# A two-layer decoder trunk on one core: fixed order of the first stage, and gemvs moved from the first FFN into the SSM

## The chip, the cores and the metric

The program runs on one core of one Trainium2 chip. A core has five engines that run side by side and meet at semaphores: TensorE (PE) for matrix products, VectorE (DVE), ScalarE (ACT) and GpSimd (POOL) for work on elements, and SyncE (SP), whose queue issues the transfers from memory in its own order. The metric is the device time of one execution in microseconds; lower is better. The kernel before takes 1230.64 us, the median of three runs between 1229.85 and 1232.05.

## The reference

A sequence of 512 tokens with 1024 channels passes two layers. Each layer has a token mixer (stick-breaking attention in layer 0, a diagonal complex state-space model, the SSM, in layer 1) and a gated feed-forward net (FFN) with a causal convolution of width 3. A vector c conditions every step: its silu times a large matrix gives shift, scale and gate vectors. All is float32.

```python
c_act = jax.nn.silu(c)
for i in range(DEPTH):
    mod = c_act @ w_mod[i] + b_mod[i]
    sh1, sc1, g1, sh2, sc2, g2 = jnp.split(mod, 6, axis=-1)
    h = modulate(rms_norm(x, norm_mix[i]), sh1, sc1)
    ...
        y = stick_breaking_attention(h, w_qkv[j], w_o_attn[j])
    ...
        y = s5_ssm(h, w_in_ssm[j], ...)
    x = x + g1[:, None, :] * y
    h = modulate(rms_norm(x, norm_ffn[i]), sh2, sc2)
    x = x + g2[:, None, :] * conv_ffn(h, w_up[i], conv_w[i], conv_b[i], w_down[i])
```

A norm divides each token by its root mean square, and `modulate` is h * (1 + scale) + shift.

## The kernel before

x lies channel-wise: eight tiles x[k] of 128 channels x 512 tokens. A float32 product is made of three products of rounded parts: `mm3` (lines 145, 148, 149) takes high x high, low x high and high x low. So each weight tile is loaded (`..._r`), copied to its high part by ACT (`..._h`, line 139), and its low part is the difference, by DVE (`..._l`, line 140). Activations have parts too: hH and hL after a norm, gH and gL after the gating of the FFN.

The stages follow one another: the first stage (load x, silu of c, squares, statistics, conditioning, and v = h times w_v over k = 0 to 7), attention in windows, the product with w_o, FFN0 in groups of 8, 8 and 6 pairs of up products, each group followed by a down projection dn_0, dn_1, dn_2, the SSM with its glu and output product, and FFN1. While FFN0 runs, POOL and the SP queue prepare the matrices of the SSM (`ssm_prep`, in pieces by `pace`).

**First stage.** `rstd_y` makes statistics: products of the sum of squares `acc` with ones (line 237), a square root on ACT, and five small DVE instructions (lines 242 to 246). `rstd_stat` puts the result on diagonals `dg` (line 254), and a product of dg with ones (line 490) broadcasts it over the partitions as `rbc`. The squares (line 1163) are summed on DVE (line 1165). Statistics are made for tokens 0 to 255, then again for 256 to 511. `norm_tile` multiplies x by the broadcast (nt, line 277), ACT makes hH and the affine value (lines 280, 281), and DVE makes hL (line 282). Shift and scale of the first norm come from gemvs: one DVE instruction multiplies 128x1024 weights by the broadcast `cact` and sums each row (`gemv_step`, line 170), two for each k, with weights in four slots `wgs`.

**Background gemvs.** All later conditioning vectors come from a list `bgq`; `bg(n)` takes the next n gemvs from it, and a vector's eight gemvs are followed by a final (`gemv_fin`, line 176). Their weights (`wg`) have two buffers, so SP can load a gemv's weights only when the one before last is done. In FFN0 gemvs stand behind pairs and in the down projections (`after`).

**Order.** A scheduler with a timeline of its own decides the order of instructions on each engine, apart from those held in program order (`keep_in_program_order`, `pe_pin`, `behind_head`). Each engine takes its list strictly in order, and the SP queue too: a load that waits for a buffer holds all loads behind it. The norms of the other stages go through `head_mm`, which starts the next stage's products on the first half of the tokens before the statistics of the second half.

## Time and profile before

| | |
|---|---|
| median of three runs | 1230.64 us |
| profiled execution | 1229.2 us |
| its span | 1227.2 us |
| PE busy | 1170.5 us (95%), 6136 instructions |
| DVE busy | 871.8 us (71%) |
| ACT busy | 562.6 us (46%) |
| POOL busy | 259.6 us (21%) |
| granted clock of PE, mean | 0.987 |

A row of the profile names an engine, the line of the kernel, the operation and its tiles (out<-in). The wait view says for whom an engine stood idle. The granted clock is a share of TensorE's full 2.4 GHz. PE is busy nearly throughout, so it is its few idle stretches, and those at a lower rate, that are looked for.

### The profile page before, as it was taken

The numbers are of one execution on the slowest core, as the hardware profiler recorded it, in microseconds if no ns is written. First come the engines' busy times: TensorE is split into PE (matmuls) and PEld (weight loads), VectorE is DVE, ScalarE is ACT, GpSimd is POOL, SyncE is SP. The second block draws the span as 40 slices with busy tenths as digits, with TensorE's granted clock in tenths as the row PEclk, the third lists the DMA queues.
The fourth block names the chain that finished last, engine by engine and source line by source line (L and its number), as shares of the span: only waits on it lengthen the run. The fifth ranks groups of instructions, "written<-read, shape, count | busy, mean of one in ns | idle before, by whom it ended". The sixth has DMA issues, their size and how long they took to land.

```text
span 1227.2 us, 16428 instructions
## 1 busy us (share of the span) xinstructions
PE 1170.5 (95%) x6136; PEld 959.5 (78%) x6136; DVE 871.8 (71%) x1305; ACT 562.6 (46%) x891; POOL 259.6 (21%) x241
## 2 busy tenths in 40 slices
PE   6999999899999999779999899999999999999997
PEld 4777776588888788558887888789888888888887
DVE  7868888747984778787678658566698458744645
ACT  7656656346642123331335657653653234422434
POOL 1000000000197986959740000000000000000003
PEclk9999999899999999979999899999999999999999
DMA  9774656521434876877767579332255436433211
GB/s 338 279 238 143 209 172 193 149 96 53 138 94 152 266 229 209 253 232 236 231 190 236 180 231 346 118 103 87 70 189 205 134 123 194 157 96 103 82 56 69
DMA packets 93395, 211.01 MB, mean 172 GB/s; under 512 B 19586, under 2 KB 39682, under 8 KB 93315
## 3 DMA queue, kind: packets, MB, share of 16 engines
q1 hardware_dynamic: 84994, 207.86, 52.8%
q10 hardware_dynamic: 8320, 2.10, 0.8%
q8 instruction: 48, 0.79, 0.3%
q14 instruction: 33, 0.26, 0.1%
HBM read 188.68 MB, written 21.24 MB: 171 GB/s over the span
## 4 chain that ended last, share of the span: by engine, by line
PE 61%; DVE 21%; POOL 5%; issue 4%; ACT 4%; DMA 4%; SPq 0%; POOLq 0%; ACTq 0%; DVEq 0%
PE up L148 8%; PE up L149 8%; PE up L145 7%; PE dn L145 4%; PE dn L148 4%; PE dn L149 4%; DVE up_l L140 4%; DVE wg L170 3%; DMA wg<-in_w_modT_dram 2%; DVE ca L396 2%; DVE ca L395 2%; DVE om L611 2%; DVE dn_l L140 1%; PE wo L145 1%; PE o L641 1%
## 5 line engine op out<-in xcount | busy, mean ns | idle before, releaser
L148 PE MATMUL up<-hL,up_h 128*128 128x512 f32 (+1 forms) x692 | 264.3, 384 | 0.3 <-DVE hL L282 0.2
L149 PE MATMUL up<-hH,up_l 128*128 128x512 f32 (+1 forms) x692 | 263.8, 383 | 0.0
L145 PE MATMUL up<-hH,up_h 128*128 128x512 f32 (+1 forms) x692 | 260.6, 384 | 1.1 <-ACT hH L280 1.1
L139 ACT ACTIVATE up_h<-up_r 128x1024 fp32r<-128x1024 f32 x84 | 88.8, 1057 | 184.9 <-PE up L148 56.8
L140 DVE TENSOR_TENSOR up_l<-up_r,up_h 128x1024 fp32r<-128x1024 f32 x84 | 121.1, 1442 | 58.7 <-ACT up_h L139 57.8
L145 PE MATMUL dn<-gH,dn_h 128*128 128x512 f32 (+1 forms) x394 | 147.6, 376 | 15.6 <-ACT gH L405 15.6
L170 DVE SCALAR_TENSOR_TENSOR wg<-wg,cact 128x1024 f32<-128x1024 f32 x96 | 128.5, 1352 | 36.4 <-DMA wg<-in_w_modT_dram 36.0
L148 PEld LDWEIGHTS up<-hL,up_h 128*128 128x128 f32 x692 | 130.0, 188 | 25.8 <-DVE hL L282 0.9
L149 PEld LDWEIGHTS up<-hH,up_l 128*128 128x128 f32 x692 | 130.1, 188 | 25.6
L145 PEld LDWEIGHTS up<-hH,up_h 128*128 128x128 f32 x692 | 128.0, 188 | 27.9 <-ACT hH L280 1.5
L148 PE MATMUL dn<-gL,dn_h 128*128 128x512 f32 (+1 forms) x394 | 147.1, 374 | 1.0 <-DVE gL L406 1.0
L149 PE MATMUL dn<-gH,dn_l 128*128 128x512 f32 (+1 forms) x394 | 146.6, 373 | 1.5 <-DVE dn_l L140 1.5
L1207 POOL TENSOR_SCALAR xa<-x,Anorm_out 128x256 f32<-128x256 f32 x7 | 5.9, 847 | 581.5 <-DVE x L311 581.3
L145 PEld LDWEIGHTS dn<-gH,dn_h 128*128 128x128 f32 x394 | 76.1, 193 | 29.4 <-ACT gH L405 16.9
L148 PEld LDWEIGHTS dn<-gL,dn_h 128*128 128x128 f32 x394 | 76.1, 193 | 14.8 <-DVE gL L406 2.2
L149 PEld LDWEIGHTS dn<-gH,dn_l 128*128 128x128 f32 x394 | 76.2, 193 | 14.5 <-DVE dn_l L140 2.3
L140 DVE TENSOR_TENSOR dn_l<-dn_r,dn_h 128x1024 fp32r<-128x1024 f32 (+1 forms) x48 | 60.0, 1259 | 33.3 <-ACT dn_h L139 33.1
L311 DVE SCALAR_TENSOR_TENSOR x<-dn,mod,x 128x512 f32<-128x512 f32 (+1 forms) x55 | 37.0, 679 | 63.2 <-PE dn L149 63.2
L139 ACT ACTIVATE dn_h<-dn_r 128x1024 fp32r<-128x1024 f32 (+1 forms) x48 | 46.7, 982 | 65.7 <-PE dn L148 40.6
L405 ACT ACTIVATE gH<-gm 128x512 fp32r<-128x512 f32 x44 | 27.7, 630 | 101.6 <-DVE gm L402 101.6
L395 DVE SCALAR_TENSOR_TENSOR ca<-up,small,ca 128x511 f32<-128x511 f32 x88 | 65.1, 742 | 7.4 <-ACT ca L394 7.4
L394 ACT ACTIVATE ca<-up,small 128x512 f32<-128x512 f32 x88 | 66.6, 761 | 7.3 <-PE up L149 7.3
(300 smaller groups left out, 2301.9 us busy)
## 6 DMA issues: line engine op xcount, KB each, us to landing
wg<-in_w_modT_dram SPq DMA_DIRECT2D x96, 512.0 KB
up_r<-in_w_up_dram SPq DMA_DIRECT2D x84, 512.0 KB
dn_r<-in_w_down_dram SPq DMA_DIRECT2D x32, 512.0 KB
wgs<-in_w_modT_dram SPq DMA_DIRECT2D x16, 512.0 KB
dn_r<-in_w_down_dram SPq DMA_DIRECT2D x16, 384.0 KB
wv_r<-in_w_v_dram SPq DMA_DIRECT2D x8, 512.0 KB
wk_r<-in_w_qk_dram SPq DMA_DIRECT2D x8, 512.0 KB
wq_r<-in_w_qk_dram SPq DMA_DIRECT2D x8, 512.0 KB
```

Of the source, the lines that this page charges most:

```text
L139: S.activation(wh[:, :n], raw[:, :n], AF.Copy)
L140: V.tensor_tensor(wl[:, :n], raw[:, :n], wh[:, :n].bitcast(F32), ALU.subtract)
L145: ins = PE.matmul(ps, ah, bh, start=start, stop=False)
L148: PE.matmul(ps, ah, bl, start=False, stop=False)
L149: PE.matmul(ps, al, bh, start=False, stop=stop)
L170: ins = V.scalar_tensor_tensor(w, w, 1.0, cact, ALU.mult, ALU.mult, accum_out=raw[:, col:col + 1])
L311: V.scalar_tensor_tensor(xs, pv, gate, xs, ALU.mult, ALU.add)
L394: S.activation(ca, ps, AF.Identity, bias=small[:, cb:cb + 1], scale=tapw[2])
L395: V.scalar_tensor_tensor(ca[:, 1:], ps[:, :T - 1], tapw[1], ca[:, 1:], ALU.mult, ALU.add)
L396: V.scalar_tensor_tensor(ca[:, 2:], ps[:, :T - 2], tapw[0], ca[:, 2:], ALU.mult, ALU.add)
L405: S.activation(gh, m, AF.Copy)
L611: V.tensor_tensor_scan(om[:, :n][:, ::-1], om[:, :n][:, ::-1], maskb[:, T - n:][:, ::-1], 1.0, ALU.mult, ALU.max)
```

## The change

**First stage.** Only squares 0 to 5 are summed on DVE (`NACC`); 6 and 7 enter the statistics as further stationary tiles. One statistics serves all 512 tokens. `cact` is copied by DVE, behind the add of k = 2, where ACT did it behind the last square. The order is written out and held on every engine: loads strictly by k, and per k on DVE nt, the gemv of the shift, the low part of w_v, the gemv of the next k's scale, hL. The first tile of w_v is split in two halves of 512 columns. Products of ones with ones (`idle`) stand on PE ahead of the statistics (7), between statistics and broadcast (4) and ahead of v (4); nobody reads their result. The load of `small` is cut in two, and the second part comes later.

**Gemvs.** FFN0 had 2 in group 0, 7 in group 1, 4 in group 2, and 8, 8 and 5 in the three down projections. Now it has 0, 3, 4, 8, 8 and 0. The eleven that are missing stand in the SSM: 2 behind the projection u, 3 and 2 in its last two rounds, and 4 in the output projection.

**Broadcast of the second half.** In `head_mm` it is now placed by `HEADB = (3, 2)`, inside the products of k = 3, where it stood ahead of the norm of k = 4.

```diff
+HEADB = (3, 2)
...
+NACC = 6
+NIDLE = (7, 4, 4)
...
-    def bg(n):
+    def bg(n, pinned=True):
...
-                gemv_step(c)
+                gemv_step(c, pinned)
...
-    def norm_tile(h, k, bc, a, b, cr=FULL):
+    def norm_tile(h, k, bc, a, b, cr=FULL, pinned=False, first=None, mid=None):
...
         hh, hl = h[0][k][:, cr], h[1][k][:, cr]
...
+        keep = pe_pin if pinned else lambda ins: None
+        keep(pin["nt"])
+        if first:
+            first()
         act = S.activation(hh, t, AF.Identity, bias=b[:, k:k + 1], scale=a[:, k:k + 1])
+        keep(act)
...
+        keep(aff)
+        if mid:
+            mid()
         dve = V.tensor_tensor(hl, u, hf, ALU.subtract)
+        keep(dve)
...
-                if cr == HALF[0] and k == HEADK - 1:
-                    rstd_bc(R, HALF[1], None, True)
                 norm_tile(h, k, R["bc"][0], a, b, cr)
-                for w, ps in hd:
+                for q, (w, ps) in enumerate(hd):
+                    if cr == HALF[0] and (k, q) == HEADB:
+                        rstd_bc(R, HALF[1], None, True)
                     mm3(ps[:, cr], wk(w, k), (h[0][k][:, cr], h[1][k][:, cr]), k == 0 and cr.start == 0, k == KD - 1)
...
                     gs.append(glu(i, i - i0, *av))
-                    if l or (i >= 6, i - i0 < 7, i - i0 < 4)[gi]:
+                    if l or i - i0 < (0, 3, 4)[gi]:
...
                 def after():
-                    if l == 0:
+                    if l == 0 and gi < 2:
...
-    def attention(acc):
+    def attention(acc, late):
...
+            def wload(v, k):
...
+                pe_pin(SP.dma_start(wgs[:, (2 * k + 1 - v) % 4, :], I["w_modT"][c * P:(c + 1) * P, :]))
+            wload(1, 0)
...
-            wv0 = load_w(I["w_v"][0:P, :], name="wv0")
...
-            def stat(cr):
-                R["ps"] = bank(aux if cr.start == 0 else mm, "stat")
-                pin["dg", cr.start] = [rstd_stat(R, cr)]
-                PE.matmul(R["bc"][cr.start][:, cr], ones, R["dg"][:, cr], start=True, stop=True)
-            stat(HALF[0])
...
+            SP.dma_start(small[:, :NMOD], I["small"][:, :NMOD])
+            wload(0, 0)
...
-            for k in range(KD):
-                with behind_head(p0) if k in (1, 2) else ExitStack():
...
-                        with behind_head(pin["sum"] if v else pin["dg", 0]):
-                            gemv_step(mcol(0, v, k), False, wgs[:, (2 * k + 1 - v) % 4, :], k > 0)
...
+            def loads(k):
+                for v in (1, 0):
+                    wload(v, k)
...
+                pin["load"] = SP.dma_start(raw, I["w_v"][k * P:(k + 1) * P, :])
+                pe_pin(pin["load"])
+                return raw
+            def high(k):
...
+                pe_pin(S.activation(w[0], raws[k], AF.Copy))
+                return w
+            def gv(v, k):
+                gemv_step(mcol(0, v, k), True, wgs[:, (2 * k + 1 - v) % 4, :], False)
...
+                pe_pin(S.activation(mod[:, c:c + 1], raw[:, c:c + 1], AF.Identity, bias=sm("b_mod", c, 1)))
+                if v:
+                    gain(k)
+            def gain(k):
...
-                for cr in HALF if k < 2 else (FULL,):
-                    if k == 0 and cr.start:
-                        with behind_head([pin["nt"]]):
-                            stat(cr)
...
-                    norm_tile(h, k, R["bc"][cr.start] if k < 2 else rb, a, mod[:, 0:KD], cr)
...
+                pe_pin(S.activation(a[:, k:k + 1], mod[:, mcol(0, 1, k):mcol(0, 1, k) + 1], AF.Identity, bias=wn, scale=wn))
+            def prods(k, w):
+                for i in vo:
...
                     mm3(vb[i], (h[0][k][:, tt * P:(tt + 1) * P], h[1][k][:, tt * P:(tt + 1) * P]),
-                        (w[0][:, nb * 512:(nb + 1) * 512], w[1][:, nb * 512:(nb + 1) * 512]), k == 0, k == KD - 1)
+                        (w[0][:, nb * 512:(nb + 1) * 512], w[1][:, nb * 512:(nb + 1) * 512]), k == 0, k == KD - 1, k == 0)
...
+            gv(1, 0)
...
+            def idle(n):
+                for q in range(n):
+                    pe_pin(PE.matmul(spare[:, :P], ones, ones, start=True, stop=True))
+            idle(NIDLE[0])
+            y = rstd_y(R, FULL, True, late)
+            idle(NIDLE[1])
+            for i in range(4):
+                V.tensor_scalar(R["dg"][:, i * P:(i + 1) * P], ident, y[:, i:i + 1], None, ALU.mult)
+            for cr in HALF:
+                pe_pin(PE.matmul(R["bc"][cr.start][:, cr], ones, R["dg"][:, cr], start=True, stop=True))
+            idle(NIDLE[2])
...
+            pe_pin(SP.dma_start(raw0, I["w_v"][0:P, :]))
...
+            def high0(q):
...
+                pe_pin(S.activation(wv0[0][:, cs], raw0[:, cs], AF.Copy))
+            def low0(q):
...
+                if q == 0:
+                    high0(1)
+                pe_pin(V.tensor_tensor(wv0[1][:, cs], raw0[:, cs], wv0[0][:, cs].bitcast(F32), ALU.subtract))
+            high0(0)
+            gv(0, 0)
...
+            vo = (0, 1, 4, 5, 2, 3, 6, 7)
...
+            raws = {1: loads(1)}
+            SP.dma_start(small[:, NMOD:], I["small"][:, NMOD:])
+            raws[2] = loads(2)
+            for q, cr in enumerate(HALF):
+                norm_tile(h, 0, R["bc"][cr.start], a, mod[:, 0:KD], cr, pinned=True, mid=lambda: low0(q))
+            for cr in HALF:
+                pe_pin(S.activation(rb[:, cr], R["bc"][cr.start][:, cr], AF.Copy))
+            prods(0, wv0)
+            w = high(1)
+            gv(1, 1)
+            for k in range(1, KD):
+                def mid():
+                    nxt[0] = high(k + 1) if k < KD - 1 else None
+                    pe_pin(V.tensor_tensor(w[1], raws[k], w[0].bitcast(F32), ALU.subtract))
+                    if k < KD - 1:
+                        gv(1, k + 1)
+                nxt = [None]
+                def first():
+                    gv(0, k)
+                    if k + 2 < KD:
+                        raws[k + 2] = loads(k + 2)
+                norm_tile(h, k, rb, a, mod[:, 0:KD], FULL, True, first, mid)
+                prods(k, w)
...
                     u_out(bi, hd[bi][1])
+                bg(2)
...
-                        V.tensor_tensor(s1[:, ri], s1[:, ri], s2[:, ri], (ALU.subtract, ALU.add)[ri])
+                        pin["comb"] = V.tensor_tensor(s1[:, ri], s1[:, ri], s2[:, ri], (ALU.subtract, ALU.add)[ri])
...
+                    if s_ >= 8:
+                        with behind_head([pin["comb"]]):
+                            bg(11 - s_, False)
...
-            bg(max(0, len([q for q in bgq if q[0] is not None]) - 24))
...
-            R = out_proj(lambda mt: I["w_os"][mt * P:(mt + 1) * P, :], gz, mcol(1, 2, 0), acc2, "wos", perm=True,
+            R = out_proj(lambda mt: I["w_os"][mt * P:(mt + 1) * P, :], gz, mcol(1, 2, 0), acc2, "wos", perm=True, after=lambda: bg(min(1, sum(q[0] is not None for q in bgq) - 24)),
...
-        PE.matmul(pc[q], ones[0:1, :], crow[:, q * 512:(q + 1) * 512], start=True, stop=True)
+        pe_pin(PE.matmul(pc[q], ones[0:1, :], crow[:, q * 512:(q + 1) * 512], start=True, stop=True))
+    late = []
     for k in range(KD):
...
-        for cr in HALF if k > 6 else (FULL,):
-            act = S.activation(sq[:, cr], x[k][:, cr], AF.Square)
-            if k:
-                add = V.tensor_tensor(acc[:, cr], acc[:, cr], sq[:, cr], ALU.add)
-                if cr.stop == T // 2:
-                    pin["sum"] = [add]
-    with behind_head([act]):
-        for q in range(2):
-            S.activation(cact[:, q * 512:(q + 1) * 512], pc[q], AF.Copy)
-    R = attention(acc)
+        S.activation(sq, x[k], AF.Square)
+        if k >= NACC:
+            late.append(sq)
+        elif k:
+            add = V.tensor_tensor(acc, acc, sq, ALU.add)
+        if k == 2:
+            with behind_head([add]):
+                for q in range(2):
+                    V.tensor_copy(cact[:, q * 512:(q + 1) * 512], pc[q])
+    R = attention(acc, late)
     for k in range(KD):
...
```

PE at the start, before; pc is the broadcast of silu(c), stat the statistics, v the products of v, in which hH_187 and hL_195 are the first channel tile:

```order
L1159 MATMUL pc_123<-crow,ones 128x512
L237 MATMUL stat<-ones,acc 128x1 x4
L490 MATMUL rbc<-dg,ones 128x256 x2
L145 MATMUL v_204<-wv_h,hH_187 128x512
L148 MATMUL v_204<-wv_l,hH_187 128x512
L145 MATMUL v_205<-wv_h,hH_187 128x512
L148 MATMUL v_205<-wv_l,hH_187 128x512
L145 MATMUL v_208<-wv_h,hH_187 128x512
L148 MATMUL v_208<-wv_l,hH_187 128x512
L145 MATMUL v_209<-wv_h,hH_187 128x512
L148 MATMUL v_209<-wv_l,hH_187 128x512
L149 MATMUL v_204<-wv_h,hL_195 128x512
```

The same place after; `spare` takes the products of ones:

```order
L1233 MATMUL pc_123<-crow,ones 128x512
L537 MATMUL spare<-ones 128x128 x7
L241 MATMUL stat<-ones,acc 128x1 x4
L241 MATMUL stat<-ones,sq 128x1 x8
L537 MATMUL spare<-ones 128x128 x4
L545 MATMUL rbc<-dg,ones 128x256 x2
L537 MATMUL spare<-ones 128x128 x4
L149 MATMUL v_232<-wv_h,hH_216 128x512
L152 MATMUL v_232<-wv_l,hH_216 128x512
L153 MATMUL v_232<-wv_h,hL_224 128x512
L149 MATMUL v_233<-wv_h,hH_216 128x512
L152 MATMUL v_233<-wv_l,hH_216 128x512
```

The statistics have three stationary tiles (acc and two sq), and the first products of v come in triples, with hL in the third, where hL stood ninth.

DVE in FFN0's group 1, from gL of pair 13 to gL and gemv of pair 14, before (ca is the convolution, gm the gated value, up_14 and dn_1 weights and products of the pair and of the down projection):

```order
L406 TENSOR_TENSOR gL_4476<-gm,gH_4475 128x512
L170 SCALAR_TENSOR_TENSOR wg_4479,modraw<-wg_4479,cact 128x1024
L140 TENSOR_TENSOR dn_1_1_l<-dn_1_1_r,dn_1_1_h 128x1024
L395 SCALAR_TENSOR_TENSOR ca_4527<-up_14_0_4502,small,ca_4527 128x511
L396 SCALAR_TENSOR_TENSOR ca_4527<-up_14_0_4502,small,ca_4527 128x510
L140 TENSOR_TENSOR dn_1_2_l<-dn_1_2_r,dn_1_2_h 128x1024
L395 SCALAR_TENSOR_TENSOR ca_4562<-up_14_1_4537,small,ca_4562 128x511
L868 SCALAR_TENSOR_TENSOR kz<-consts,small,kz 128x16
L396 SCALAR_TENSOR_TENSOR ca_4562<-up_14_1_4537,small,ca_4562 128x510
L402 TENSOR_TENSOR gm<-ca_4527,ca_4562 128x512
L406 TENSOR_TENSOR gL_4570<-gm,gH_4569 128x512
L170 SCALAR_TENSOR_TENSOR wg_4573,modraw<-wg_4573,cact 128x1024
```

The same stretch after:

```order
L419 TENSOR_TENSOR gL_4469<-gm,gH_4468 128x512
L144 TENSOR_TENSOR dn_1_1_l<-dn_1_1_r,dn_1_1_h 128x1024
L408 SCALAR_TENSOR_TENSOR ca_4517<-up_14_0_4492,small,ca_4517 128x511
L409 SCALAR_TENSOR_TENSOR ca_4517<-up_14_0_4492,small,ca_4517 128x510
L144 TENSOR_TENSOR dn_1_2_l<-dn_1_2_r,dn_1_2_h 128x1024
L408 SCALAR_TENSOR_TENSOR ca_4552<-up_14_1_4527,small,ca_4552 128x511
L939 SCALAR_TENSOR_TENSOR kz<-consts,small,kz 128x16
L409 SCALAR_TENSOR_TENSOR ca_4552<-up_14_1_4527,small,ca_4552 128x510
L415 TENSOR_TENSOR gm<-ca_4517,ca_4552 128x512
L419 TENSOR_TENSOR gL_4560<-gm,gH_4559 128x512
L144 TENSOR_TENSOR dn_1_3_l<-dn_1_3_r,dn_1_3_h 128x1024
```

The two gemvs (wg) behind the two gL are gone, and all else keeps its order.

DVE at the end of the last down projection, where the next norm's sum of squares (acc) is formed, before (x is the residual update, win the weights of the SSM's projection):

```order
L311 SCALAR_TENSOR_TENSOR x_78<-dn_2_0_5664,mod,x_78 128x512
L170 SCALAR_TENSOR_TENSOR wg_5707,modraw<-wg_5707,cact 128x1024
L311 SCALAR_TENSOR_TENSOR x_79<-dn_2_1_5686,mod,x_79 128x512
L140 TENSOR_TENSOR dn_2_5_l<-dn_2_5_r,dn_2_5_h 128x768
L140 TENSOR_TENSOR dn_2_6_l<-dn_2_6_r,dn_2_6_h 128x768
L311 SCALAR_TENSOR_TENSOR x_80<-dn_2_2_5726,mod,x_80 128x512
L140 TENSOR_TENSOR dn_2_7_l<-dn_2_7_r,dn_2_7_h 128x768
L216 TENSOR_TENSOR acc<-acc,sq 128x512
L170 SCALAR_TENSOR_TENSOR wg_5717,modraw<-wg_5717,cact 128x1024
L311 SCALAR_TENSOR_TENSOR x_81<-dn_2_3_5758,mod,x_81 128x512
L216 TENSOR_TENSOR acc<-acc,sq 128x512
L170 SCALAR_TENSOR_TENSOR wg_5749,modraw<-wg_5749,cact 128x1024
```

And after:

```order
L324 SCALAR_TENSOR_TENSOR x_78<-dn_2_0_5650,mod,x_78 128x512
L324 SCALAR_TENSOR_TENSOR x_79<-dn_2_1_5672,mod,x_79 128x512
L144 TENSOR_TENSOR dn_2_5_l<-dn_2_5_r,dn_2_5_h 128x768
L144 TENSOR_TENSOR dn_2_6_l<-dn_2_6_r,dn_2_6_h 128x768
L324 SCALAR_TENSOR_TENSOR x_80<-dn_2_2_5706,mod,x_80 128x512
L220 TENSOR_TENSOR acc<-acc,sq 128x512
L144 TENSOR_TENSOR dn_2_7_l<-dn_2_7_r,dn_2_7_h 128x768
L220 TENSOR_TENSOR acc<-acc,sq 128x512
L324 SCALAR_TENSOR_TENSOR x_81<-dn_2_3_5735,mod,x_81 128x512
L144 TENSOR_TENSOR win_l<-win_r,win_h 128x1024 x2
L220 TENSOR_TENSOR acc<-acc,sq 128x512
L144 TENSOR_TENSOR win_l<-win_r,win_h 128x1024
```

Three gemvs have left this piece, and two more stood behind it, so the updates and sums stand closer.

## Rows read from the trace of the kernel before

**Rows 1.** Waits of PE over the span: who waited for whom, total us, times, longest.
```profile
PE dn L145 <- ACT gH L405: 15.6, 3, 12.1
PE stat L237 <- DVE acc L1165: 4.5, 1, 4.5
PE stat L237 <- DVE acc L216: 3.9, 2, 3.0
PE rbc L490 <- DVE dg L254: 3.8, 2, 2.9
...
PE dn L149 <- DVE dn_l L140: 1.5, 2, 1.3
```

**Rows 2.** Timeline of PE, first stage; start, us, engine, line, operation, count, idle before.
```profile
11.64 1.86 PE L237 MATMUL stat<-ones,acc 128*128 128x1 f32 x8 [4.49 <-DVE acc L1165]
...
19.19 0.99 PE L145 MATMUL v<-wv_h,hH 128*128 128x512 f32 x1
...
20.83 0.63 PE L148 MATMUL v<-wv_l,hH 128*128 128x512 f32 x1
...
24.63 0.39 PE L145 MATMUL v<-wv_h,hH 128*128 128x512 f32 x1
24.86 0.40 PE L148 MATMUL v<-wv_l,hH 128*128 128x512 f32 x1
...
39.00 2.12 PE L149 MATMUL v<-wv_h,hL 128*128 128x512 f32 x8 [2.75 <-DVE hL L282]
...
68.17 0.39 PE L145 MATMUL k<-hH,wk_h 128*128 128x512 f32 x1
```

**Rows 3.** Timeline of ACT, first stage: the last six squares.
```profile
7.31 3.41 ACT L1163 ACTIVATE sq<-x 128x512 f32<-128x512 f32 x6 [0.89 <-DMA x<-in_xT_dram]
```

**Rows 4.** Timeline of DVE, first stage.
```profile
13.92 0.48 DVE L254 TENSOR_SCALAR dg<-consts,ny 128x128 f32<-128x128 f32 x2
...
29.33 1.22 DVE L140 TENSOR_TENSOR wv_l<-wv_r,wv_h 128x1024 fp32r<-128x1024 f32 x1
30.47 1.22 DVE L170 SCALAR_TENSOR_TENSOR wgs<-wgs,cact 128x1024 f32<-128x1024 f32 x1
...
31.61 1.22 DVE L170 SCALAR_TENSOR_TENSOR wgs<-wgs,cact 128x1024 f32<-128x1024 f32 x1
...
38.26 0.69 DVE L282 TENSOR_TENSOR hL<-nt,hH 128x512 fp32r<-128x512 f32 x1
```

**Rows 5.** Tile wgs: for what its engine sat idle before it, us and times.
```profile
  DMA wgs<-in_w_modT_dram: 0.2, 1
```

**Rows 6.** Timeline of DVE, down projection 0 and group 1 of FFN0.
```profile
410.21 2.04 DVE L170 SCALAR_TENSOR_TENSOR wg<-wg,cact 128x1024 f32<-128x1024 f32 x1 [5.54 <-DMA wg<-in_w_modT_dram]
...
475.81 1.22 DVE L170 SCALAR_TENSOR_TENSOR wg<-wg,cact 128x1024 f32<-128x1024 f32 x1
...
527.54 1.21 DVE L170 SCALAR_TENSOR_TENSOR wg<-wg,cact 128x1024 f32<-128x1024 f32 x1
```

**Rows 7.** Groups by line on DVE, 475 to 527; count, busy us, mean ns, idle before.
```profile
L170 DVE SCALAR_TENSOR_TENSOR wg<-wg,cact 128x1024 f32<-128x1024 f32 x4 | 7.1, 1769 | 0.0
```

**Rows 8.** Timeline of the SP queue, down projection 0.
```profile
401.80 0.59 SPq L169 DMA_DIRECT2D wg<-in_w_modT_dram  x1
```

**Rows 9.** Timeline of PE, in dn_1 and at the end of dn_2.
```profile
526.66 0.79 PE L145 MATMUL dn<-gH,dn_h 128*128 128x512 f32 x1 [12.09 <-ACT gH L405]
...
676.53 0.98 PE L237 MATMUL stat<-ones,acc 128*128 128x1 f32 x4 [3.02 <-DVE acc L216]
```

**Rows 10.** Groups by line on DVE, 654 to 677.
```profile
L170 DVE SCALAR_TENSOR_TENSOR wg<-wg,cact 128x1024 f32<-128x1024 f32 x5 | 6.1, 1217 | 0.0
```

**Rows 11.** Timeline of DVE, last rounds of the SSM.
```profile
781.57 0.69 DVE L1088 TENSOR_TENSOR hL<-z,hH 128x512 fp32r<-128x512 f32 x1 [3.85 <-ACT hH L1087]
```

**Rows 12.** Windows: busy and count of PE, PEld, DVE, ACT, POOL; clock, DMA, GB/s.
```profile
676.00:680.00 4.00, 3.47 (x16) 3.50 (x17) 1.96 (x9) 0.57 (x2) 0.00 (x0) 0.50 0.52 165
860.00:866.00 6.00, 4.81 (x32) 4.19 (x33) 4.30 (x11) 5.66 (x10) 0.00 (x0) 1.00 0.23 66
```

43 lines of the change are left out of this document (18 added, 25 removed).

## The prediction

> **What bounds the kernel now.** I read the waits of TensorE (PE) first, because PE is busy nearly all the time and only its idle stretches and its slow stretches can be won back. The list is short [rows 1]: the first down product of a group waits three times for the gated value gH, 15.6 us, of which one wait is 12.1; the statistics of the first stage wait 4.5 for the sum of squares; statistics of later norms wait 3.9; the broadcast of the first stage waits 3.8; a down product waits 1.3 for its low part. Then I read PE's own rows at each of these places, and VectorE's (DVE) rows just ahead, to see what kept the producer. Three places matter.
>
> First stage: the statistics start at 11.64, the first product of v at 19.19, and the first product of k, that is the end of v, at 68.17 [rows 2]. At full rate products start 0.23 apart (24.63, 24.86), and 8 blocks x 8 k x 3 = 192 of them take 192 x 0.227 = 43.5 us. The stage takes 68.17 - 19.19 = 49.0. The missing 5.5 are one wait of 2.75 for hL at 39.00 and about 2.7 because the products up to about 24 are slow (0.63 each against 0.39).
>
> FFN0, second group: PE stands still for 12.09 until 526.66 [rows 9]. DVE is not idle then; it works through a chain of conv, gating and weight splitting, and behind each gated value stands a gemv (a product of 128x1024 with the conditioning, reduced along the row).
>
> SSM head: PE waits 3.02 at 676.53 for the last sum of squares [rows 9], and afterwards its granted clock is 0.50 for four us [rows 12], which is 1.2 of 2.4 GHz.
>
> **The change, part A: first stage.** Squares 6 and 7 no longer go through the DVE sum; they are products of their own in the statistics, which serve both halves at once. Their price is 24 small PE instructions instead of 8. The eight took 1.86, 0.23 each [rows 2]; four took 0.98 at the lower clock [rows 9]. So the 24 cost 5.5 at that rate and about half, 2.8, if the PE is at full rate by then; 8 of them stand behind the last square, which ends at 7.31 + 3.41 = 10.72 [rows 3]. DVE now has five adds and two copies of 512 columns ahead of the last sum instead of eight adds, so the sum is there at about 10.3 (an estimate). The statistics end at 10.3 + 2.9 = 13.2, or 15.8 at the low rate. From there: before, dg began at 13.92 [rows 4], 1.35 after the first four of the eight instructions; four dg instead of two, 0.24 each, are 0.9; one gemv 1.15; nt and hH of a half together 0.9 (an estimate from the 0.69 of a full hL, [rows 4]). That is 4.3 from the end of the statistics, so v starts at 17.5, or at 20.1. The first triple needs hL at once, which I price at 0.5, and the step to k=1 at 1.0.
>
> The products of ones (7, 4 and 4) fill PE's waits ahead of v and cost nothing there, being shorter than the waits. What they buy is the rate: v at 0.227 from its first product. Per k, DVE has two gemvs (1.15 from start to start), wv_l 1.14, nt and hL 0.6 each (0.69 less the overlap) [rows 4], 4.6 in all, under PE's 24 x 0.227 = 5.44; so the fixed order has 0.8 per k in hand, and the 2.75 wait has no cause left: there DVE had taken splits and gemvs of later k ahead of hL, and in the fixed order of the new kernel two gemvs and one split, 3.4, lie between nt and hL of a k, while PE has 16 products, 3.6, that don't need hL. End of v: 17.5 + 0.5 + 1.0 + 43.5 = 62.5; one more us for loads gives 63.5. **Term A: -4.7**, from -7 (no hitches, v at 17) to -1.7 (v at 20.1, slow for as long as before). The loads of the q and k weights now stand behind the last wgs; the conversion has them by the end of v, and I put this at zero, with 1 either way. The small tensor's second part is first used in FFN0 and costs nothing.
>
> On the rate of the first products the Trainium skill ("TensorE: Matmul & The Clock Gate", What's actually happening) says that a lower clock is the resting state and activity releases it. The trace shows such a change of rate at 24, though at 19.19 PE had just run statistics and broadcasts; by the page the products of ones give back the 2.7, and by the opposite reading A would be -2.
>
> **Part B: gemvs out of FFN0.** 34 gemvs were in FFN0, 23 stay. Group 0 loses two (PE had no wait there), group 1 keeps three of seven (pairs 8, 9, 10), the last down projection loses all five. In group 1 the removed gemvs stood behind pairs 11 to 14, three of them ahead of the gH that ends the 12.09. Four gemvs in the stretch took 7.1 together [rows 7], the one of pair 10 that stays 1.22 [rows 6], so the three are worth 5.9; the fourth, 1.21 [rows 6], stands ahead of the next wait for gH. With the loads of the gemvs in the first down projection issued earlier, DVE loses its idle 5.54 at 410.21 [rows 6], and PE the 1.3 on a low part [rows 1]. Against this stands the final of a modulation vector that moves into pair 10, 0.2 to 1.3; I take 0.7. Sum: -5.9 - 1.2 - 1.3 + 0.7 = -7.7; I leave 0.7 of it out because the wait's other producers (ACT's copies) then weigh more, so **term B: -7**. The gap stays near 6, so the slow clock behind it stays too and is no gain. Bounds: -9.5, if also POOL's chain and the loads on SP behind it come earlier, and -3, if each removed gemv is only worth its undisturbed 1.2 and the final costs its most.
>
> The mean of those gemvs is 1.77 [rows 7], where the same instruction alone takes 1.22 [rows 6]; POOL prepares the SSM in this stretch. The Trainium skill ("SBUF — State Buffer", Who interferes with whom) has DVE and GpSimd lock a shared pair of ports for a whole instruction. By that page the next DVE instruction inherits the wait, the three gemvs give 3 x 1.22 = 3.7 instead of 5.9, and the time would be 1217.6; I count this with the first rival below.
>
> **Part C: SSM head.** Between 655 and 676 DVE is without a pause, and five gemvs, 6.1 in all [rows 10], stand in it. Without them the sum of squares ends soon after the last down product, as in the other head that waits for it, where the wait is 3.9 - 3.0 = 0.9 [rows 1]; behind the wait in FFN1's head the clock stays at 1.00 [rows 12]. The wait of 3.02 becomes about 1, and the four us at half clock give back 2. **Term C: -4**, from -6 to -1 (the chain through ACT's squares sets it).
>
> **Part D: what the SSM takes in.** Eleven gemvs of 1.22 plus finals. Two follow the projection u, with weights loaded far ahead; five stand in the last two rounds, where DVE idles 3.85 ahead of hL at 781.57 [rows 11]; four lie in the output projection. PE has work meanwhile. The danger is the order: behind the gemvs DVE has the splits of the glu weights and hL, and the SP queue has the output weights behind the gemvs' loads. **Term D: +0.5**, 0 to +4 (three gemvs on the path).
>
> **Part E: later broadcast.** On PE the broadcast of the second half stands where it stood in every head: the same number of rows behind the first one. Zero.
>
> **Sum.** -4.7 - 7 - 4 + 0.5 = -15.2. The profiled execution took 1229.2, which gives 1214.0; the median lies 1.4 above it, so the forecast is 1215.4.
>
> **The rivals.** (1) The wait in FFN0 re-forms: the chain is then set by ACT, by POOL's instructions and the loads on SP that wait for them, or by the port lock, and B is only -3. For it: DVE has pauses in this stretch, while it waits for ACT. Against: they are in series with the gemvs. 1215.4 + 4 = 1219.4. (2) The first stage doesn't warm: A is -1.7, 1218.4. For it: 24 more small instructions sit on the path. (3) The SSM head keeps its wait: C is -1, 1218.4. (4) The change doesn't do what it says, and every part comes out at its poor bound: -1.7 - 3 - 1 + 4 = -1.7, 1228.9. For it: the four bounds have one cause in common, that other engines set these places; against: DVE is the releaser by name in two of three. (5) Slower: the first stage becomes bound by its loads. Loads for k+2 are issued only when the second gemv of k is done, strictly in order. A period is then (time from issue to landing + 4.6 of DVE) / 2. In FFN0 a load issued at 401.80 [rows 8] kept a gemv waiting until 410.21 [rows 6], 8.4; two more loads of the step follow at 1.6 each, 11.6. The period is 8.1, seven steps lose 7 x (8.1 - 5.44) = 18.6, and the time is 1234. It decides from 7.6 per step on, that is 10.6 from issue to landing. Against it: in the first stage DVE waited for these loads 0.2 in all [rows 5].
>
> **How the numbers follow.** Forecast 0.52; (1) 0.20; (2) 0.10; (3) 0.08; (4) 0.05; (5) 0.05. The first four keep to 1208 to 1225, with their own spread of some 4 and with two together; about 0.18 lies outside. A difference under 0.2%, 2.5 us, can't be told from none. Faster 0.90, same 0.05, slower 0.05.
>
> **What would show it.** A: first v near 17.5 at 0.23 apart, no wait over 1 at hL, first k product near 63.5. B: the wait for gH near 6 instead of 12, DVE without gemvs between the pairs 11 and 15, and no wait for a gemv's load in the first down projection. C: the statistics of the SSM head within 1.2 of the down product ahead, and a clock of 1.00 behind it. D: no new PE wait over 0.5 between 760 and 850. I am wrong if the wait for gH stays over 9, if DVE shows pauses for wgs loads, or if the SSM gets longer by more than 2.

## The result: 1215.85 us, and the profile after

The changed kernel takes 1215.85 us in the median of four runs (1214.38 to 1218.89), the kernel before beside it 1230.24. The ratio is 0.9887 with an interval of 0.9862 to 0.9912, 14 us less; 1215.4 was forecast, and the range was 1208 to 1225. A second measurement with other runs gave 1215.46 and 0.9894 (0.9879 to 0.9908).

The profiled execution, 1218.9 with a span of 1216.5, is the slowest of the four. The page after, its share of busy time and its slices:

```profile
span 1216.5 us, 16497 instructions
...
PE 1176.2 (97%) x6182; PEld 964.7 (79%) x6182; DVE 874.3 (72%) x1298; ACT 560.6 (46%) x886; POOL 257.3 (21%) x241
...
PEclk9989999899999999989999999999999999999999
```

The span less PE's busy time is 56.7 before and 40.3 now: 16 us of PE's idle time are gone. The span fell by 10.7 only, since PE's busy time is up by 5.7; the products of ones, whose result nobody reads, alone are 6.1. Who still waits, on PE (who waited for whom, total us, times, longest):

```profile
PE dn L149 <- ACT gH L418: 10.4, 3, 7.2
PE t L694 <- DVE om L682: 4.1, 5, 1.8
...
PE z L676 <- DVE q_nt L656: 3.3, 2, 2.0
...
PE z L676 <- DVE q_sq L656: 1.4, 1, 1.4
PE pv L1065 <- DMA u<-sU: 1.3, 1, 1.3
...
PE stat L241 <- DVE acc L220: 0.9, 1, 0.9
...
PE v L149 <- ACT hH L288: 0.7, 1, 0.7
...
PE stat L241 <- DVE acc L1241: 0.2, 1, 0.2
PE rbc L545 <- DVE dg L543: 0.2, 1, 0.2
```

Against [rows 1] the wait for gH has gone from 15.6 to 10.4, its longest from 12.1 to 7.2; the first stage's 4.5 and 3.8 are 0.2 each, with products of ones in their place; the waits for sums of squares are down to one of 0.9. New is 1.3 for u in the SSM. The waits of attention are not new. The same view of the kernel before has them too, smaller:

```profile
PE t L623 <- DVE om L611: 2.1, 4, 0.8
PE z L605 <- DVE q_sq L585: 2.0, 2, 1.4
PE z L605 <- DVE q_nt L585: 1.8, 2, 1.1
```

So the wait for om went from 2.1 to 4.1, and q from 3.8 to 4.7. Of q's 4.7 the first pair has 1.43 and 1.31; the other 2.03 lie near the end of attention.

PE's first stage, which answers to [rows 2]:

```profile
7.06 3.36 PE L537 MATMUL spare<-ones 128*128 128x128 f32 x14
10.62 1.05 PE L241 MATMUL stat<-ones,acc 128*128 128x1 f32 x8 [0.21 <-DVE acc L1241]
11.54 1.93 PE L241 MATMUL stat<-ones,sq 128*128 128x1 f32 x16
...
15.21 2.07 PE L545 MATMUL rbc<-dg,ones 128*128 128x256 f32 x4 [0.19 <-DVE dg L543]
...
17.93 0.48 PE L149 MATMUL v<-wv_h,hH 128*128 128x512 f32 x1
...
24.70 0.50 PE L149 MATMUL v<-wv_h,hH 128*128 128x512 f32 x1 [0.69 <-ACT hH L288]
...
62.91 0.39 PE L149 MATMUL k<-hH,wk_h 128*128 128x512 f32 x1
```

The products of ones (spare) run until 10.4, the 24 statistics instructions take 2.8 in all, v starts at 17.93 at full rate, the one wait left in v is 0.69 at k = 1, and v ends at 62.91. The wait for gH and u's late start, which answer to [rows 9], and the first SSM product behind it:

```profile
519.89 0.79 PE L149 MATMUL dn<-gH,dn_h 128*128 128x512 f32 x1 [7.16 <-ACT gH L418]
...
666.86 0.58 PE L241 MATMUL stat<-ones,acc 128*128 128x1 f32 x4
...
707.17 1.15 PE L1065 MATMUL pv<-u,pB 128*64 128x64 f32 x32 [1.27 <-DMA u<-sU]
```

The statistics of the SSM head, 3.02 late before, don't wait at all, and no window there has a lower clock. The windows (length; busy time and count of PE, PEld, DVE, ACT and POOL; then granted clock, DMA share and GB/s):

```profile
664.00:668.00 4.00, 4.00 (x35) 3.85 (x34) 2.67 (x8) 1.36 (x4) 0.00 (x0) 1.00 0.31 123
668.00:672.00 4.00, 4.00 (x35) 3.94 (x33) 2.78 (x11) 0.91 (x3) 0.00 (x0) 1.00 0.02 4
672.00:676.00 4.00, 3.77 (x31) 3.42 (x30) 2.75 (x7) 4.00 (x9) 0.00 (x0) 1.00 0.88 277
```

Both profiles side by side, by the start of the same instruction on PE:

| point | before | after | difference |
|---|---|---|---|
| first product of v | 19.19 | 17.93 | -1.3 |
| first product of k (end of v) | 68.17 | 62.91 | -5.3 |
| statistics behind the output projection of attention | 275.83 | 276.43 | +0.6 |
| end of the long wait for gH | 526.66 | 519.89 | -6.8 |
| end of the last wait for gH | 653.38 | 646.82 | -6.6 |
| first product of u | 684.38 | 672.21 | -12.2 |
| first product pv of the SSM | 718.05 | 707.17 | -10.9 |
| statistics in FFN1's head | 846.35 | 835.46 | -10.9 |

Read by stages: first stage -5.3, attention **+5.9**, FFN0 -7.2, SSM head -5.6, SSM +1.3, the rest 0. The second stage stood in the sum at zero. What it lost can be read from windows. The first of these three is the kernel before, the others are the changed kernel; they are all the stretches of attention with a granted clock of 0.50:

```profile
221.55:228.38 6.83, 6.12 (x17) 4.39 (x19) 6.20 (x12) 1.28 (x4) 0.00 (x0) 0.50 0.63 214
```

```profile
82.00:88.83 6.83, 5.96 (x16) 4.89 (x17) 5.30 (x9) 5.13 (x10) 0.00 (x0) 0.50 0.34 99
218.54:228.78 10.24, 7.29 (x21) 5.18 (x23) 8.31 (x14) 3.54 (x8) 0.00 (x0) 0.50 0.46 151
```

PE's idle time in attention went from 8.14 to 10.47, 2.3 more. Its busy time at half the rate went from 6.12 to 13.25; half of these 7.1 is lost, 3.6 (an estimate from these rows). Together that is the 5.9.

So the open questions were where the first stage's gain goes, whether FFN0 and the SSM head are worth what they look like, and what the products of ones do.

### The profile page after: what moved, and what is told of

Its sections match the earlier page's. It is cut to its first block, busy times and chain, and to the rows that moved or that the text cites. A ratio compares the mean times of both kernels' runs of the same rounds, so it can differ in the third digit from the quotient of the medians.

```text
span 1216.5 us, 16497 instructions
## 1 busy us (share of the span) xinstructions
PE 1176.2 (97%) x6182; PEld 964.7 (79%) x6182; DVE 874.3 (72%) x1298; ACT 560.6 (46%) x886; POOL 257.3 (21%) x241
## 4 chain that ended last, share of the span: by engine, by line
PE 68%; DVE 13%; DMA 5%; POOL 5%; ACT 4%; issue 3%; SPq 1%; POOLq 0%; DVEq 0%; ACTq 0%
PE up L152 10%; PE up L153 10%; PE up L149 10%; PE dn L153 5%; PE dn L149 5%; PE dn L152 5%; DVE up_l L144 2%; PE o L712 1%; DVE wgs L174 1%; PE wo L149 1%; PE wos L149 1%; PE wos L153 1%; DMA wg<-in_w_modT_dram 1%; PE wo L153 1%; PE wo L152 1%
## 5 line engine op out<-in xcount | busy, mean ns | idle before, releaser
L143 ACT ACTIVATE up_h<-up_r 128x1024 fp32r<-128x1024 f32 x84 | 88.8, 1057 | 181.4 <-DMA up_r<-in_w_up_dram 63.7
L149 PE MATMUL dn<-gH,dn_h 128*128 128x512 f32 (+1 forms) x394 | 146.2, 372 | 10.4 <-ACT gH L418 10.4
L174 DVE SCALAR_TENSOR_TENSOR wg<-wg,cact 128x1024 f32<-128x1024 f32 x96 | 125.8, 1325 | 37.0 <-DMA wg<-in_w_modT_dram 36.7
L324 DVE SCALAR_TENSOR_TENSOR x<-dn,mod,x 128x512 f32<-128x512 f32 (+1 forms) x55 | 37.1, 679 | 62.9 <-PE dn L153 62.9
```

What stands on the lines that cost most here:

```text
L143: S.activation(wh[:, :n], raw[:, :n], AF.Copy)
L149: ins = PE.matmul(ps, ah, bh, start=start, stop=False)
L174: ins = V.scalar_tensor_tensor(w, w, 1.0, cact, ALU.mult, ALU.mult, accum_out=raw[:, col:col + 1])
L324: V.scalar_tensor_tensor(xs, pv, gate, xs, ALU.mult, ALU.add)
```

## The experiments

**Halves of the change.** The gemvs alone are these edits in the kernel before, whose first stage stays:

```diff
-                    if l or (i >= 6, i - i0 < 7, i - i0 < 4)[gi]:
+                    if l or i - i0 < (0, 3, 4)[gi]:
...
-                    if l == 0:
+                    if l == 0 and gi < 2:
...
+                bg(2)
...
+                    if s_ >= 8:
+                        with behind_head([pin["comb"]]):
+                            bg(11 - s_, False)
...
-            bg(max(0, len([q for q in bgq if q[0] is not None]) - 24))
...
+            R = out_proj(lambda mt: I["w_os"][mt * P:(mt + 1) * P, :], gz, mcol(1, 2, 0), acc2, "wos", perm=True, after=lambda: bg(min(1, sum(q[0] is not None for q in bgq) - 24)),
```

The first stage alone is the changed kernel with these edits undone, and with the broadcast of the second half at its old place (the expectation speaks of the new place; part E below shows that the two give the same order).

> Only the first stage of the change (and the new place of the later broadcast); all gemvs stand where they stood before. Theory 1, the parts add up and what the first stage wins passes through attention: v ends 5 earlier (k product near 63) and the whole takes about 1225.5, 4.7 under the kernel before. Rival, attention gives it back: in the trace of the changed kernel the end of v came 5.3 earlier but the statistics behind the output projection 0.6 later; then v ends at 63 here too, those statistics start near 276, and the time is within 1 of 1230. FFN0's wait for gH stays near 12, the SSM head's near 3.

Measured: 1228.7 beside 1229.13, ratio 1.000 (0.9986 to 1.0015). The end of v came 2.1 earlier in its profile, the statistics behind attention 0.9 earlier, but the last wait for gH 0.4 later, and the span is 0.7 shorter. The first stage alone is worth nothing that can be measured; theory 1 falls for it, in this form. The rival is only half right: v ended at 66.1 and not at 63, and attention gave back 1.2 of the 2.1.

The gemvs alone:

> Only the gemvs moved (pairs 11 to 14, the last down projection, group 0, into the SSM); the first stage is the one before. Theory 1: 7 from group 1, 4 from the SSM head, 0.5 lost: about 1220, with the first stage's 5 missing against the changed kernel. Rival, attention swallows the first stage's gain: the same time as the changed kernel, 1216 to 1217. The wait for gH near 7, for the SSM head's sum below 1.2, and one wait for u in the SSM near 1.3, if that comes from the moved gemvs' loads.

Measured: 1220.38, ratio 0.9935 (0.9909 to 0.996), and again, beside the changed kernel:

> Only the gemvs moved, once more, beside the changed kernel on the same chip. Alone the new first stage gained 0.4 and the moved gemvs 8.7, together 13 to 14. Theory 1, the first stage's gain arrives only when FFN0's chain on DVE no longer swallows it: 3 to 5 slower than the changed kernel in this call. Rival, the two are simply additive and the 4 was scatter: within 1.5 of the changed kernel.

1218.63, ratio 0.9924 (0.9912 to 0.9936); the changed kernel, measured beside it:

> The changed kernel once more, beside the three below. In three profiles of its first stage the first product of k came at 62.9, 66.1 and 65.9, since the small statistics instructions ran at the full rate once and at half of it twice. Theory 1, the rate at the start differs from one execution to the next: a fourth profile lies near 63 or near 66, not in between. The time is 1214 to 1217. If it comes out 1218 to 1220, the first stage adds nothing to the moved gemvs and the result of the changed kernel was a good draw.

1215.46, ratio 0.9894 (0.9879 to 0.9908). The gemvs are worth 8.7 to 9.8, and the first stage on top of them 0.003, 3.2 us by the medians, its interval from 1 to 6. That it brings 3 there and 0 alone is at the edge of what the intervals allow (0.997 against 1.000, each about 0.002), so a dependence is likely, not shown. The profile of this second measurement of the changed kernel differs from the first mainly in one stage: attention took 207.6 from the first product of k to the statistics, where the first profile has 213.5 and the kernel before 207.7; its time, 1212.65, is the shortest of its four.

**FFN0's second group.** Pairs 11 to 14 keep their gemvs:

```diff
-                    if l or i - i0 < (0, 3, 4)[gi]:
+                    if l or i - i0 < (0, 7, 4)[gi]:
```

> The changed kernel, but pairs 11 to 14 of FFN0 keep their gemvs; the output projection of the SSM loses its four. By the prediction this undoes 7: wait for gH near 12, chain of gated values in group 1 longer by 5.7 to 6.6, total 1221 to 1223. By the rival that the gain of the group is only the undisturbed 1.2 of each (the next instruction inherits the wait behind POOL): 3.7 to 4.9, 1219 to 1220. If the gemvs in the SSM cost much, this run gets some of it back: below 1219.

Measured: 1221.55, ratio 0.9946 (0.9925 to 0.9968) against 0.9894: 6.1 us by the medians, within the forecast of 1221 to 1223, and the intervals lie apart. The wait is back in full. PE at the second group's down products in this run:

```profile
522.31 0.80 PE L149 MATMUL dn<-gH,dn_h 128*128 128x512 f32 x1 [12.09 <-ACT gH L418]
...
533.44 0.79 PE L149 MATMUL dn<-gH,dn_h 128*128 128x512 f32 x1 [3.18 <-ACT gH L418]
```

12.09 and 3.18, where the changed kernel has 7.16 and 2.18. The long wait differs from one profile to the next: it is 5.7 to 10.1 in the eleven profiles in which these gemvs are moved, and 12.0 to 12.1 in the three in which they stay. That the output projection got four gemvs less gave nothing back: from the first pv to the statistics of FFN1's head it takes 128.3 with them and without.

**SSM head.** The last down projection keeps its five gemvs:

```diff
-                    if l == 0 and gi < 2:
+                    if l == 0:
```

> The changed kernel, but the last down projection keeps five gemvs; the output projection of the SSM has none, FFN1 one less. By the prediction this undoes 4 (in the trace it looks like 5.6 from the wait for gH to the start of u): the wait for the sum of squares of the SSM head back at 3, the clock at 0.5 to 0.7 behind it, total 1219 to 1221. Rival, the head is bound elsewhere: no wait over 1.2 there and the total within 1.5 of the changed kernel.

Measured: 1218.71, ratio 0.9925 (0.991 to 0.9941): 3.3 us by the medians, just below the 1219 to 1221 forecast. The wait is back, and the low clock behind it. PE at the statistics:

```profile
667.03 0.58 PE L241 MATMUL stat<-ones,acc 128*128 128x1 f32 x4 [2.93 <-DVE acc L220]
```

And the window behind it (columns as in the windows above):

```profile
669.00:672.40 3.40, 3.40 (x17) 3.22 (x16) 1.18 (x4) 0.42 (x1) 0.00 (x0) 0.50 0.03 8
```

2.93 of waiting, and a granted clock of 0.50 for 3.4 us, where the changed kernel shows 1.00. From the last wait for gH to u it takes 30.1 here and 25.4 in the changed kernel, 4.7 more.

**Products of ones.** None at all:

```diff
-NIDLE = (7, 4, 4)
+NIDLE = (0, 0, 0)
```

> The changed kernel without the fifteen products of ones, nothing else. If these give the rate at which v starts: v products about 0.43 apart until some 4 to 5 us after the start, statistics at 0.2 an instruction or slower, the first product of v at 19 to 20 instead of 17.9, the first product of k 3 to 5 later than 62.9. If the order alone did it: the first product of k within 1 of 62.9. On the total, 1 to 4 over the changed kernel by the first, nothing by the second; nothing by either if attention swallows the first stage's gain.

Measured: 1217.72, ratio 0.9907 (0.9874 to 0.994). And once more:

> The changed kernel without any product of ones, once more with more rounds; the first look gave 0.991 (0.987 to 0.994). If the products of ones are worth what the early end of v shows (65.8 without, 62.9 to 63.9 with, four times of six): ratio 0.991 to 0.992, 2 to 3 over the changed kernel. If only the order counts: 0.989 to 0.990. The statistics at half rate in this profile too, and v at 0.43 apart until 4 us after its start.

1217.17, ratio 0.9903 (0.9884 to 0.9922), against 0.9887 and 0.9894 with them: 1 to 2 us for them, inside the intervals. The edit does more than it says: without the products of ones the scheduler puts attention's instructions on PE and ACT in the order of the kernel before, and with them in another. And what v gains is gone at the statistics behind attention, which come at 273.0 and 273.5 without them and at 271.2 to 276.4 in the six profiles with them and the old place of vn (see below). So this pair of runs doesn't price the rate by itself. Their profiles have v's end at 65.8 and 66.2, with v at half rate for its first four us; with seven products of ones it lay at 62.9, 63.0, 63.7 and 63.9 in four profiles and at 65.4, 65.9 and 66.1 in three. PE in one of the late ones (the first stage alone), whose program is the same up to there as in the early one shown above:

```profile
7.15 3.36 PE L537 MATMUL spare<-ones 128*128 128x128 f32 x14
11.34 1.87 PE L241 MATMUL stat<-ones,acc 128*128 128x1 f32 x8 [0.83 <-DVE acc L1238]
13.07 3.55 PE L241 MATMUL stat<-ones,sq 128*128 128x1 f32 x16
...
21.80 0.66 PE L149 MATMUL v<-wv_h,hH 128*128 128x512 f32 x1
```

The eight and the sixteen statistics instructions take 1.87 and 3.55 here, 1.05 and 1.93 above: half rate against full rate. To see whether PE's rest of 0.83 ahead of 11.34 decides it, ten products instead of seven:

```diff
-NIDLE = (7, 4, 4)
+NIDLE = (10, 4, 4)
```

> The changed kernel with ten products of ones ahead of the statistics instead of seven. Where the statistics ran at half rate (two of six profiles of this first stage), TensorE had stood idle 0.8 ahead of them, since the last sum came at 11.1 to 11.3; where they ran at full rate it had stood 0.2 to 1.0. Theory 1, a longer run of these products makes the full rate the rule: statistics (24 instructions) within 3.2 us, first product of v by 19, first product of k by 64.5; in the mean 1 under the changed kernel, 1213 to 1216. Rival, the rate doesn't depend on these three: half rate may come up again, time as the changed kernel or 0.7 above it.

Measured: 1215.45, ratio 0.9894 (0.987 to 0.9918), the same as the changed kernel. Its profile:

```profile
7.03 4.64 PE L537 MATMUL spare<-ones 128*128 128x128 f32 x20
11.46 1.77 PE L241 MATMUL stat<-ones,acc 128*128 128x1 f32 x8
13.09 3.55 PE L241 MATMUL stat<-ones,sq 128*128 128x1 f32 x16
...
20.94 0.50 PE L149 MATMUL v<-wv_h,hH 128*128 128x512 f32 x1
```

No rest at all, from 7.03 on, and the statistics still at half rate. The run with both edits below had the same twenty instructions and its statistics at full rate (1.10 and 1.93). So the rest isn't what decides; the rate rises early in some executions and late in others behind the same work. Theory 1 falls. What the products of ones do change is when the full rate comes to stay: by the clock records of the traces at 17.1 to 22.2 in all nine profiles with them, and at 23.6 to 25.0 in all five without, the kernel before among these. Where the rate rose early, in five of the nine (at 10.2 to 11.9), it fell back to half at 13.6 to 15.3, although PE was busy with the statistics and the next products of ones then; so these don't hold it.

**The start of attention.** In the changed kernel DVE finishes vn (v less its shifted copy, eight subtractions) among the parts of the first pair's q. DVE there:

```profile
77.63 0.69 DVE L624 TENSOR_TENSOR vn<-vn,vs 128x512 f32<-128x512 f32 x1 [0.66 <-DMA vs<-sV]
78.24 1.22 DVE L144 TENSOR_TENSOR wk_l<-wk_r,wk_h 128x1024 fp32r<-128x1024 f32 x1
79.37 0.68 DVE L624 TENSOR_TENSOR vn<-vn,vs 128x512 f32<-128x512 f32 x1
80.09 0.68 DVE L656 TENSOR_TENSOR q_sq<-q,q_sq 64x512 fp32r<-64x512 f32 x1
80.80 1.29 DVE L624 TENSOR_TENSOR vn<-vn,vs 128x512 f32<-128x512 f32 x2
82.13 0.69 DVE L656 TENSOR_TENSOR q_nt<-q,q_nt 64x512 fp32r<-64x512 f32 x1
```

q_sq and q_nt, for which PE waits, stand behind one subtraction and behind two. In the kernel before one stood ahead of each, and PE waited 0.61 and 0.71. vn is needed only one window later. The eight go behind q:

```diff
-            for i in range(8):
-                nb, tt = divmod(i, 4)
-                dst = vn[:, tt, nb * 512:(nb + 1) * 512]
-                V.tensor_tensor(dst, dst, vs[i], ALU.subtract)
...
-                            V.tensor_tensor(t[other], ps[own], t[own].bitcast(F32), ALU.subtract)
+                            pin["q"] = V.tensor_tensor(t[other], ps[own], t[own].bitcast(F32), ALU.subtract)
...
             for u in proj(0):
                 u()
+            for i in range(8):
+                nb, tt = divmod(i, 4)
+                dst = vn[:, tt, nb * 512:(nb + 1) * 512]
+                with behind_head([pin["q"]]):
+                    V.tensor_tensor(dst, dst, vs[i], ALU.subtract)
```

> The changed kernel, but the eight subtractions that finish vn on DVE stand behind the q of the first head pair instead of among its parts. In the changed kernel TensorE waits 1.4 and 1.3 there for q_sq and q_nt, and the clock is 0.77 in 75 to 90. If this order on DVE is where the first stage's gain goes: these two waits below 0.5 each, the clock at 1.00, the statistics behind the output projection 3 to 5 earlier, the total 1211 to 1213. If the gain is lost elsewhere (the end of attention, 210 to 230, or by chance from run to run): within 1.5 of the changed kernel.

Measured: 1213.28, ratio 0.988 (0.9846 to 0.9913). Once more:

> The eight subtractions of vn behind the first pair's q, once more with more rounds. The first look gave 0.988 (0.985 to 0.991) against 0.989 of the changed kernel, so it may be 0 to 3 better. If the waits of 1.3 to 2.7 for q_sq and q_nt count in full: ratio 0.987 to 0.988. If not: 0.989 to 0.990.

1213.04, ratio 0.9864 (0.9843 to 0.9885). Measured beside it, the run with ten products of ones, whose time is that of the changed kernel, had 1215.45. The two waits are gone from this place, and the stretch of 76 to 90 is full. That window in the changed kernel:

```profile
76.00:90.00 14.00, 11.26 (x40) 8.85 (x40) 10.55 (x16) 7.17 (x13) 0.00 (x0) 0.76 0.46 156
```

And with vn late:

```profile
76.00:90.00 14.00, 14.00 (x68) 11.83 (x67) 11.83 (x18) 9.09 (x16) 0.00 (x0) 1.00 0.62 229
```

PE is busy 11.26 of 14 at a clock of 0.76 in the one, 14.00 at 1.00 in the other. In the other profiles with the old place of vn and the new first stage PE was busy 11.82 to 12.69 there, at 1.00 in all but one (0.88); with vn late 14.00 in all three. The last run has both edits:

> Both edits: ten products of ones, and the eight subtractions of vn behind the first pair's q on DVE. If both places are real and independent: 1211 to 1213, ratio to the kernel before 0.986 to 0.988, v's end by 64.5 and no wait for q_sq or q_nt over 0.5. If the next chain swallows what is won ahead of it, as FFN0's did with the first stage alone: 1215, as the changed kernel.

1215.25, ratio 0.9881 (0.986 to 0.9901): no better than the order of vn alone. With vn late, attention took 207.3 to 207.5 in three profiles; with the products of ones and the old place of vn it took 207.6 to 213.5 in six, 210.0 in the mean. In the five profiles without products of ones (the kernel before, the gemvs alone and the two above), where the scheduler left the old order, it took 206.5 to 208.7. So the wait at q is shown to go, and the order of vn is likely one place that gives the first stage's gain back. That it pays on the whole isn't shown. It is 2.4 us by the medians beside the run with ten products of ones, but the intervals overlap (0.9843 to 0.9885 and 0.987 to 0.9918), the run with both edits doesn't bear it out, and the statistics behind attention come at 271.8 to 273.2, inside the 271.2 to 276.4 of the old place. The profile of the second run with vn late is 9.3 shorter than that of the run with ten products of ones beside it; only 2.9 of this arise ahead of these statistics and 5.9 in FFN0, where both run the same instructions in the same order. By its median the late vn alone is the fastest version here.

## Why the prediction was right, point by point

**Part A, -4.7 at the end of v.** The steps held in the result's profile: first v at 17.93 for 17.5, the 24 statistics instructions at 2.8 for 2.8, end of v at 62.91 for 63.5, one wait of 0.69 where 1.0 had been priced, and no wait for loads. The lower bound that I kept, v at 20.1 with the statistics at half rate, is no remote case: it came in three of seven profiles (v at 20.3 to 21.8, end at 65.4 to 66.1). What I had called the rule was a draw. The step that failed is a sentence at the end of the part: all that it has for the attention behind v is the loads of the q and k weights, at "zero, with 1 either way". Attention lengthened by 5.9 in the result's profile, by -0.1 to 3.2 in the other five of this order, and of the 4.7 nothing arrives in the kernel with the first stage alone, 3 (1 to 6) on top of the gemvs. The cause is not the loads of the q and k weights that I weighed, since PE never waits for them. What the result's profile has in place of the zero is 2.3 more of PE's idle time, most of it behind DVE (q of the first pair 1.3 before and 2.7 now; om 2.1 and 4.1), and 3.6 from more work at half the rate. What I had not seen is that the change also moves instructions inside attention. The scheduler decides there by its own timeline, and with the products of ones in the first stage it orders PE, DVE and ACT otherwise: two subtractions of vn come between q_sq and q_nt where one stood. The waits at the first pair's q go when vn is late; the longer waits for om stay, and an attention held in its old order wasn't tried, so how much of the loss is the order's is not shown.

The Trainium skill ("TensorE: Matmul & The Clock Gate", What's actually happening) says that the array rests at the lower clock and that activity releases it. The runs agree in direction: without products of ones v began at half rate in all five profiles, with them in three of nine. The page also says that the moment varies from run to run, by about half a microsecond. The runs show far more: behind the same instructions the first rise on record stands at 10.3 in one execution and at 22.2 in another, which I had left out of the sum.

**Part B, -7.** From the statistics behind attention to the last wait for gH the profile has -7.2, and putting the four gemvs of group 1 back costs 6.1. PE's idle time between these two points fell from 19.6 to 12.6, while its busy time at half rate stayed (8.7 and 9.0), as forecast. The long wait is 7.16, where "near 6" was forecast; the sign of being wrong, over 9, came in three of eleven profiles with these gemvs moved (9.8 to 10.1). The chain itself, from the gated value of pair 11 to that of pair 14, was 40.9 before (39.4 to 40.9 in three profiles) and is 34.3 now, 6.6 less; it is 34.1 to 34.7 in eight profiles and 36.5 to 37.2 in the same three, 3.7 to 4.3 less. That is the other end, near the three gemvs at 1.22 each.

The Trainium skill ("SBUF — State Buffer", Who interferes with whom) says that DVE and GpSimd lock a shared pair of ports and that whichever comes second blocks. What I read from it, that the next DVE instruction inherits the wait, fits the three profiles (the dn_l in this stretch take 1.9 to 2.0 there in the mean) and not the other eight (1.5 to 1.7); no run separates it from other causes.

One step of the sum failed: DVE did not lose its idle time for a gemv's load in the first down projection. It waited 11.86 and 5.54 there before, and once, for longer, now:

```profile
409.44 2.09 DVE L174 SCALAR_TENSOR_TENSOR wg<-wg,cact 128x1024 f32<-128x1024 f32 x1 [13.94 <-DMA wg<-in_w_modT_dram]
```

PE's 1.3 on a low part behind it is nevertheless down to 0.4.

**Part C, -4.** The profile shows -5.6 from gH to u; undone, that stretch grows by 4.7 and the total by 3.3. The mechanism was right (wait of 3.02 to none, clock 1.00). In the profile both terms were larger than the 2 each that I gave them: the wait gave all of its 3.0, and 5.8 us of work at half rate became work at full rate, 2.9. The interval of the total (1 to 6) holds all of these sizes.

**Part D, +0.5.** The result's profile has +1.3: the first pv comes 34.96 behind the first u where it came 33.67, with a wait of 1.27 for u, and nothing behind it. In the other profiles with the moved gemvs it is +0.1 to +1.3, with a wait for u of 0.4 to 1.4 in all but one, and with none where no gemv stands behind u. The five gemvs in the last rounds and the four in the output projection are covered, as forecast. The wait is for u's way through memory; whether the loads of the two gemvs behind u delay it wasn't tried apart.

**Part E, zero.** The runs with the gemvs alone have the broadcast at its old place. From the statistics behind attention to the end their traces show the order of the changed kernel on all five engines (in one of them two neighbouring DVE instructions are swapped), so this part changes nothing.

**The total** is right to half a us, and part of that is luck. The change was forecast at -15.2; it measured -14.4 in the result and -13.0 in the second measurement. The profile has it by terms that partly cancel: B at 7.2 for 7 and C at 5.6 for 4, while A arrived at 0 to 3 instead of 4.7 and D cost up to 0.8 more. Undone one by one beside the changed kernel, the first stage is worth 3.2, group 1 6.1 and the SSM head 3.3, together 12.6 of the 13.0; by these medians A, at 3.2 for 4.7, is the term that was furthest off. The rivals: the first stage not warming (2) is true of part of the executions; the wait that re-forms (1) of three of eleven profiles; the SSM head keeping its wait (3), all parts at their poor bound (4), and loads in lockstep (5), were wrong, the loads of wgs made DVE wait once, 1.0 at 11.57, ahead of v.

## What to carry to other kernels

A stage that ends earlier is worth only what the next stage's slowest chain lets through: price the instruction for which the next stage waits first, and the order of the engine that makes it, before counting the gain. Where a scheduler orders by a timeline, compare its order in all later stages too: here fifteen products whose result nobody reads changed the order of the next stage. Work that several other engines' timing hangs on is best taken off the engine whose chain ends last, here eleven reductions from DVE's busiest stretch into one where it idles, and this was worth about seven tenths of the total (0.0076 of 0.0106, measured side by side). Where a term rests on a clock that is just rising or just falling, take several profiles, since one shows a draw.
